# Grouped-query values: each product over 128 keys split into two products over 64 keys, on the upper and lower halves of the array, with the two halves summed after PSUM

## The chip, the cores and the metric

One core of one Trainium2 chip runs the whole program. The metric is device time in microseconds (us) of one execution; lower is better.

## The reference, cut to what matters

The program is a two-layer encoder trunk on 256 tokens of width 1024. Layer 0 uses a dilated attention mixer, layer 1 the windowed grouped-query mixer that the change touches. Each layer runs a SwiGLU block before and after its mixer, and a gated embedding at its end.

```
def reference(x, p, norm_g, ffn_wi, ffn_wo, ple_proj, ple_gate, a_wqkv, a_wo, b_wqkv, b_wo, b_sink, ...):
    for i in range(DEPTH):                      # DEPTH = 2
        h = h + 0.5 * rms_norm(swiglu(rms_norm(h, g[0]), ffn_wi[i, 0], ffn_wo[i, 0]), g[1])
        ...                                     # mixer: dilated (layer 0), window_gqa_mixer (layer 1)
        h = h + 0.5 * rms_norm(swiglu(rms_norm(h, g[4]), ffn_wi[i, 1], ffn_wo[i, 1]), g[5])
        ...                                     # gated embedding

def window_gqa_mixer(h, wqkv, wo, sink, cos, sin):   # 16 heads of 64, 4 key/value heads
    q, k, v = split(h @ wqkv)                        # rope on q and k
    s = q @ k.T / 8, only where |i - j| <= 128
    pr = exp(s - m); den = sum(pr) + exp(sink - m)
    o = (pr @ v) / den                               # the product in question
    return o @ wo
```

## The kernel before

The tokens lie in two tiles of 128 (t = 0, 1). In the grouped-query mixer (`mixer_b`) a unit is one token tile and four heads; there are eight units, (t, pr) with pr = 0 to 3. A unit goes through four steps:

- `scores`: 12 matmuls (L567) of 64 array rows each, alternately on rows 0 to 63 and 64 to 127, into two banks of the pool `psy`. `soft` then adds the mask and takes the row minimum on VectorE (L580), and takes the exponential with its sum on ScalarE (L583).
- `trans`: 16 transposes (`transpose_p`, L340), again 64 rows each and alternating, into two banks of the pool `pst`. ScalarE copies one bank and VectorE the other to `pT` (L343). `pT` has the 128 keys of a key tile on its partitions, and 128 queries in its columns.
- `values`: for each of four heads and each of two key tiles, one fp32 matmul (L602) with `pT` as weights (128 keys x 128 queries) and 64 columns of `V` as the moving side. The trace has two records for each fp32 matmul, so a unit has 16 L602 records; this document calls them the unit's burst. They go to columns 0 to 255 of one bank of the pool `psa`.
- the evacuation: VectorE multiplies by the reciprocal of the denominator (L605), TensorE transposes the result twice (L610) into columns 256 to 511 of the same bank, ScalarE casts it to the output tile `oT` (L73, the high part) and VectorE subtracts (L74, the low part). The bank is free after that subtraction.

The pool `psa` has two banks. A unit takes one of them, so two units alternate. `attend` writes the units down in order, with the scores two units ahead and the transposes one ahead. Output projections (`out_proj`, L205: 48 matmuls of 512 columns for a token tile) are written after unit 4 for t = 0, and at the end for t = 1. A scheduler then sets the order of each engine from that text, with the matmuls of one `scores`, one `transpose_p` kept in their written order. Each engine runs its own list strictly in order. After the mixer the second SwiGLU block of layer 1 follows (L194, L241, L205).

Of the kernel before, what the change touches and what calls it, by code (L numbers as in the profile page):

```python
# [12 lines left out]
ALU = mybir.AluOpType  # L13

P = 128
# [4 lines left out]
DH = 64  # L20
# [17 lines left out]
def trunk_kernel(ctx, tc, x, p, norm_g, ffn_wi, ffn_wo, ple_proj, ple_gate, a_wqkv, a_wo,  # L38
                 b_wqkv, b_wo, b_sink, rope, mask_a, mask_b, out):
    nc = tc.nc  # L40
# [13 lines left out]
    E = mybir.EngineType  # L54
# [7 lines left out]
    def w2_tile(shape, dt=F32):  # L62
        return w2.tile(shape, dt, name="w2t", tag="w2t")

    def m4_tile(shape, dt=F32):
        return m4.tile(shape, dt, name="m4t", tag="m4t")

    def bank(which, shape=(P, 512)):
        pl = {"y": ps_y, "a": ps_a, "t": ps_t}[which]
        return pl.tile(list(shape), F32, name=f"ps{which}", tag=f"ps{which}")  # L70

    def split(dst_hi, dst_lo, src):
        nc.scalar.copy(dst_hi, src)  # L73
        nc.vector.tensor_tensor(dst_lo, src, dst_hi.bitcast(F32), ALU.subtract)  # L74
# [433 lines left out]
    def mixer_b(acts, gb, row):  # L508
# [12 lines left out]
        V = m4_tile([P, 2, 256])  # L521
# [73 lines left out]
        def values(t, pr):  # L595
            a, ih = pr // 2, pr % 2
            pT, rd = pTs.pop((t, pr))
            o_ps = bank("a")
            for n in range(4):
                for kt in range(2):  # L600
                    kv = 2 * a + n % 2
                    nc.tensor.matmul(o_ps[:, n * DH:(n + 1) * DH], pT[:, 2 * n + kt, :],  # L602
                                     V[:, kt, kv * DH:(kv + 1) * DH], start=(kt == 0), stop=(kt == 1))
            o_n = w2_tile([P, 256])
            nc.vector.tensor_tensor(o_n.rearrange("p (n d) -> p n d", d=DH),  # L605
                                    o_ps[:, 0:256].rearrange("p (n d) -> p n d", d=DH),
                                    rd.unsqueeze(2).broadcast_to([P, 4, DH]), ALU.mult)
            pt = o_ps[:, 256:512]
            for i in range(2):
                nc.tensor.transpose(pt[:, i * P:(i + 1) * P], o_n[:, i * P:(i + 1) * P], ident)  # L610
            if ih == 0:
                oT[t, a] = m4_tile([P, 2, 4, P], F32R)
            o = oT[t, a]
            split(o[:, 0, 2 * ih:2 * ih + 2, :].rearrange("p n q -> p (n q)"),
                  o[:, 1, 2 * ih:2 * ih + 2, :].rearrange("p n q -> p (n q)"), pt)
# [22 lines left out]
        def mid():  # L638
            flush()
            score(0)  # L640

        b(1, mid)
        return attend(units, score, trans, values, 1, [lambda k=k: wo_pair(k) for k in range(8)],
                      lambda t: [oT[t, 0], oT[t, 1]], gb, row, flush)

# [82 lines left out]
    start = ExitStack()  # L728
# [83 lines left out]
```

## Time and profile before

| | |
|---|---|
| median of 3 runs | 1082.66 us (1082.51 to 1082.91) |
| the profiled execution | 1083.56 us, of which the span of the trace is 1081.7 us |
| TensorE matmul busy | 1055.7 us, 98% of the span |
| VectorE busy | 692.6 us, 64% |
| ScalarE busy | 565.1 us, 52% |
| mean granted TensorE clock | 0.992 of 2.4 GHz |

The trace's times are microseconds from the start of the span. PE is TensorE's matmul side, PEld its weight loads, DVE is VectorE, ACT is ScalarE. The units' bursts lie between 803.5 and 845 us. Matmuls overlap, so the distance between the starts of two matmuls says more than the duration of one. Nothing below goes by the median alone: a term is found in the profiled execution, and then added to the median.

### The profile page before, as it was taken

How to read it: one execution, taken by the hardware profiler on the slowest of the kernel's cores; microseconds unless marked ns; L12 is line 12 of the kernel's file. 1: busy time of each engine (PE TensorE's matmuls, PEld its weight loads, DVE VectorE, ACT ScalarE, POOL GpSimd, SP SyncE). 2: the span in 40 equal slices, each digit the busy share in tenths (PEclk: the TensorE clock that was granted, in tenths of full speed). 3: DMA queues.
4: the chain of work that ended last, by engine and by line, in shares of the span. 5: the costliest groups of instructions: out<-in, count | busy, mean ns of one | idle time of the engine just before them, and what ended most of it. 6: DMA issues, size and time to landing. Idle time of an engine off the chain costs nothing.

```text
span 1081.7 us, 15005 instructions
## 1 busy us (share of the span) xinstructions
PE 1055.7 (98%) x5254; PEld 862.8 (80%) x5254; DVE 692.6 (64%) x1499; ACT 565.1 (52%) x888; POOL 0.7 (0%) x6
## 2 busy tenths in 40 slices
PE   7999999999999999999999999999999999999996
PEld 5888888778877888888887888888778878888885
DVE  5765554875577856566588654555986866557465
ACT  5654443575576645455456543544674564446343
POOL 0000000000000000000000000000000000000000
PEclk8999999999999999999999999999999999999998
DMA  8965655556550666576444756555651566567501
GB/s 256 298 208 159 212 169 200 175 178 193 175 156 12 202 216 195 160 248 211 160 138 152 232 169 206 180 171 158 179 151 40 168 213 195 168 209 242 200 1 39
DMA packets 130236, 189.05 MB, mean 175 GB/s; under 512 B 9441, under 2 KB 100321, under 8 KB 130161
## 3 DMA queue, kind: packets, MB, share of 16 engines
q1 hardware_dynamic: 130160, 188.10, 54.7%
q8 instruction: 41, 0.67, 0.2%
q14 instruction: 35, 0.28, 0.1%
HBM read 187.02 MB, written 1.05 MB: 174 GB/s over the span
## 4 chain that ended last, share of the span: by engine, by line
PE 92%; DVE 3%; ACT 3%; issue 1%; DMA 1%; SPq 1%; DVEq 0%; ACTq 0%
PE psa L194 55%; PE psy L205 29%; PE pst L241 2%; PE psa L602 1%; PE psa L670 1%; PE pst L147 1%; DMA raw<-in_ffn_wi_dram 1%; PE pst L317 1%; ACT w L88 1%; PE pst L340 1%; ACT w2t L583 1%; PE psa L188 1%; ACT w2t L402 1%; DVE w2t L401 0%; PE psy L326 0%
## 5 line engine op out<-in xcount | busy, mean ns | idle before, releaser
L194 PE MATMUL psa<-w,hgT 128*128 128x512 f32 x2664 | 633.1, 393 | 0.5 <-ACT m4t L380 0.5
L194 PEld LDWEIGHTS psa<-w,hgT 128*128 128x128 f32 x2664 | 494.7, 188 | 103.2 <-ACT m4t L380 0.9
L91 DVE TENSOR_TENSOR w<-raw,w 128x512 fp32r<-128x512 f32 x672 | 435.4, 688 | 168.3 <-ACT w L88 159.6
L88 ACT CAST w<-raw 128x1024 fp32r<-128x1024 f32 (+1 forms) x340 | 352.7, 1042 | 197.0 <-issue 82.8
L205 PE MATMUL psy<-w,w2t 128*128 128x512 f32 x1056 | 260.2, 398 | 2.5 <-ACT w2t L73 2.5
L205 PEld LDWEIGHTS psy<-w,w2t 128*128 128x128 f32 x1056 | 194.4, 188 | 47.4 <-ACT w2t L73 5.4
L232 ACT ACTIVATE w2t<-psa,small 128x256 f32<-128x256 f32 x88 | 41.8, 475 | 155.3 <-PE psa L194 151.0
L233 DVE SCALAR_TENSOR_TENSOR w2t<-psa,small,w2t 128x256 f32<-128x256 f32 x88 | 42.3, 481 | 112.7 <-ACT w2t L232 112.7
L74 DVE TENSOR_TENSOR w2t<-pst,w2t 128x256 fp32r<-128x256 f32 x88 | 36.6, 416 | 9.2 <-ACT w2t L73 9.2
L73 ACT CAST w2t<-pst 128x256 fp32r<-128x256 f32 x88 | 32.2, 366 | 10.1 <-PE pst L241 9.9
L73 ACT CAST hgT<-w2t 128x512 fp32r<-128x512 f32 x32 | 19.5, 620 | 33.7 <-DVE w2t L149 33.5
L205 PE MATMUL psy<-w,m4t 128*128 128x512 f32 x144 | 35.4, 397 | 0.0
L241 PEld LDWEIGHTS pst<-ident,w2t 128*128 128x128 f32 x176 | 24.4, 139 | 13.4 <-issue 1.8
L241 PE MATMUL pst<-ident,w2t 128*128 128x128 f32 x176 | 33.5, 271 | 1.6 <-DVE w2t L233 1.5
L205 PEld LDWEIGHTS psy<-w,m4t 128*128 128x128 f32 x144 | 26.3, 188 | 5.5 <-DVE small L401 0.2
L149 DVE TENSOR_TENSOR w2t<-pst,gcol 128x512 f32<-128x512 f32 x32 | 21.1, 684 | 10.5 <-PE pst L147 10.5
L115 ACT ACTIVATE w2t<-psy 128x512 f32<-128x512 f32 x24 | 14.2, 595 | 18.1 <-DVE w2t L167 18.0
L205 PE MATMUL psy<-w,hgT 128*128 128x512 f32 x96 | 23.4, 392 | 0.0
L172 DVE SCALAR_TENSOR_TENSOR h<-w2t,small,h 128x512 f32<-128x512 f32 x32 | 22.6, 748 | 0.4
L205 PE MATMUL psy<-m4t,hgT 128*128 128x512 f32 x96 | 22.6, 389 | 0.0
L74 DVE TENSOR_TENSOR hgT<-w2t,hgT 128x512 fp32r<-128x512 f32 x32 | 21.4, 687 | 0.9 <-ACT hgT L73 0.4
L167 DVE TENSOR_TENSOR w2t<-psy,gb 128x512 f32<-128x512 f32 x24 | 16.5, 686 | 7.4 <-PE psy L205 7.4
(91 smaller groups left out, 535.0 us busy)
## 6 DMA issues: line engine op xcount, KB each, us to landing
raw<-in_ffn_wi_dram SPq DMA_DIRECT2D x352, 256.0 KB, 4.0
raw<-in_ffn_wo_dram SPq DMA_DIRECT2D x88, 512.0 KB, 4.8
raw<-in_a_wqkv_dram SPq DMA_DIRECT2D x36, 512.0 KB, 4.6
raw<-in_ple_gate_dram SPq DMA_DIRECT2D x16, 512.0 KB, 4.1
raw<-in_b_wqkv_dram SPq DMA_DIRECT2D x12, 512.0 KB, 4.1
gb<-in_norm_g_dram SPq DMA_DIRECT2D x8, 512.0 KB, 4.6
raw<-in_b_wo_dram SPq DMA_DIRECT2D x16, 256.0 KB, 5.8
raw<-in_a_wo_dram SPq DMA_DIRECT2D x4, 512.0 KB, 4.6
```

The costliest lines, as they stand in the source:

```text
L73: nc.scalar.copy(dst_hi, src)
L74: nc.vector.tensor_tensor(dst_lo, src, dst_hi.bitcast(F32), ALU.subtract)
L88: nc.scalar.copy(w[0][:, i:i + step], raw[:, i:i + step])
L91: nc.vector.tensor_tensor(w[1][:, c], raw[:, c], w[0][:, c].bitcast(F32), ALU.subtract)
L149: nc.vector.tensor_tensor(hg, pt.rearrange("p (k q) -> p k q", k=4), gcol[:, 4 * q:4 * q + 4, self.row].unsqueeze(2).broadcast_to([P, 4, P ...
L167: nc.vector.tensor_tensor(g, y[i], gb[:, i * 512:(i + 1) * 512], ALU.mult)
L172: nc.vector.scalar_tensor_tensor(h[t][:, s], yg[i], r, h[t][:, s], ALU.mult, ALU.add)
L194: nc.tensor.matmul(ps, lhs(a, xh, 2 * c + k), ws[c][wh][:, k * 512:(k + 1) * 512], start=(c == 0 and k == 0 and n == 0), stop=(c == 3 and ...
L205: nc.tensor.matmul(y[half], lhsf(k, xh), ws[k][wh][:, half * 512:(half + 1) * 512], start=(first and k == 0 and i == 0), stop=(last and k ...
L232: nc.scalar.activation(su[:, 0, :], ps[:, 0:256], AF.Silu, scale=acts[t].rstd)
L233: nc.vector.scalar_tensor_tensor(su[:, 1, :], ps[:, 256:512], acts[t].rstd, su[:, 0, :], ALU.mult, ALU.mult)
L241: nc.tensor.transpose(pt[:, f * P:(f + 1) * P], su[:, 1, f * P:(f + 1) * P], ident)
```

## The change

```
-            o_ps = bank("a")
-            for n in range(4):
-                for kt in range(2):
-                    kv = 2 * a + n % 2
-                    nc.tensor.matmul(o_ps[:, n * DH:(n + 1) * DH], pT[:, 2 * n + kt, :],
-                                     V[:, kt, kv * DH:(kv + 1) * DH], start=(kt == 0), stop=(kt == 1))
+            o_ps = [bank("a") for _ in range(2)]
+            with tc.manual_schedule(engines={E.PE}):
+                for n in range(4):
+                    for kt in range(2):
+                        for hf in range(2):
+                            kv = 2 * a + n % 2
+                            rows = slice(64 * hf, 64 * hf + 64)
+                            nc.tensor.matmul(o_ps[hf][:, n * DH:(n + 1) * DH], pT[rows, 2 * n + kt, :],
+                                             V[rows, kt, kv * DH:(kv + 1) * DH], start=(kt == 0), stop=(kt == 1))
+            o_h = w2_tile([P, 256])
+            nc.scalar.copy(o_h, o_ps[0][:, 0:256])
             o_n = w2_tile([P, 256])
-            nc.vector.tensor_tensor(o_n.rearrange("p (n d) -> p n d", d=DH),
-                                    o_ps[:, 0:256].rearrange("p (n d) -> p n d", d=DH),
+            nc.vector.tensor_tensor(o_n, o_ps[1][:, 0:256], o_h, ALU.add)
+            nc.vector.tensor_tensor(o_n.rearrange("p (n d) -> p n d", d=DH), o_n.rearrange("p (n d) -> p n d", d=DH),
                                     rd.unsqueeze(2).broadcast_to([P, 4, DH]), ALU.mult)
+            o_ps = o_ps[0]
             pt = o_ps[:, 256:512]
```

Each matmul over 128 keys becomes two over 64 keys, the first on array rows 0 to 63 into one bank, the second on rows 64 to 127 into the other. Both banks of `psa` now belong to one unit. ScalarE copies the first half's sum to SBUF (the copy, L608 of the changed kernel), VectorE adds the second half to it (the add, L610), and multiplies by the reciprocal in SBUF (the multiplication, L611). The transposes of the result (now L616) go to the first bank, as before to the one bank. The matmuls are now L605.

TensorE from unit 1's burst to that of unit 2, before:

```order
L602 MATMUL psa<-m4t,pT 128x64 x8
L340 MATMUL pst<-ident,w2t 128x64 x16
L602 MATMUL psa<-m4t,pT 128x64
L610 MATMUL psa<-ident,w2t 128x128 x2
L602 MATMUL psa<-m4t,pT 128x64 x7
L567 MATMUL psy<-m4t 128x256 x11
```

The same place after the change, on to the burst of unit 2 (the fifteen after the last L567):

```order
L605 MATMUL psa<-m4t,pT 128x64 x15
L340 MATMUL pst<-ident,w2t 128x64 x16
L605 MATMUL psa<-m4t,pT 128x64
L567 MATMUL psy<-m4t 128x256 x6
L616 MATMUL psa<-ident,w2t 128x128 x2
L567 MATMUL psy<-m4t 128x256 x5
L340 MATMUL pst<-ident,w2t 128x64
L567 MATMUL psy<-m4t 128x256
L605 MATMUL psa<-m4t,pT 128x64 x15
```

Before, unit 2's matmuls start right behind the transposes, and unit 1's L610 stands among them. After, only the first matmul of unit 2 stands ahead of unit 1's transposes of the result (it takes the bank that the add frees); the other fifteen stand behind them, since the second one takes the bank that the transposes write.

VectorE around the evacuation of unit 1, after the change (the ISA rows of L580 are the masked minimum and the reading of its result):

```order
L610 TENSOR_TENSOR w2t<-psa,w2t 128x256
L576 COPY w2t<-nsk 128x2
L580 ISA w2t,quad<-psy,msk,nsk 128x256
L580 ISA quad 128x1
L611 TENSOR_TENSOR w2t<-w2t,quad 128x256
L580 ISA w2t,quad<-psy,msk,nsk 128x256
L580 ISA quad 128x1
L576 COPY w2t<-nsk 128x2
L580 ISA w2t,quad<-psy,msk,nsk 128x256
L580 ISA quad 128x1
L74 TENSOR_TENSOR m4t<-psa,m4t 128x256
```

A copy of L576 and one L580 stand between the add and the multiplication, two more L580 between the multiplication and the subtraction that frees the bank. Before, one multiplication from PSUM (L605) stood in place of the add and the multiplication.

TensorE from the transposes of unit 4's result to the end of the first output projection, before:

```order
L602 MATMUL psa<-m4t,pT 128x64 x8
L205 MATMUL psy<-w,m4t 128x512 x7
L610 MATMUL psa<-ident,w2t 128x128 x2
L205 MATMUL psy<-w,m4t 128x512 x39
L567 MATMUL psy<-m4t 128x256 x12
```

The same place after, from the transposes of unit 3's result on:

```order
L605 MATMUL psa<-m4t,pT 128x64
L205 MATMUL psy<-w,m4t 128x512 x3
L616 MATMUL psa<-ident,w2t 128x128 x2
L205 MATMUL psy<-w,m4t 128x512 x5
L605 MATMUL psa<-m4t,pT 128x64 x15
L205 MATMUL psy<-w,m4t 128x512 x6
L616 MATMUL psa<-ident,w2t 128x128 x2
L205 MATMUL psy<-w,m4t 128x512 x32
L567 MATMUL psy<-m4t 128x256 x12
```

Eight of the output projection's matmuls have moved ahead of unit 4's burst (two stand ahead of both pieces in either kernel).

## Rows read from the trace of the kernel before

**Rows 1.** Stages: length, busy PE, PEld, DVE, ACT, POOL (counts), clock, DMA share, GB/s.

```profile
803.50:834.00 30.50, 30.06 (x269) 25.63 (x270) 20.47 (x76) 16.34 (x54) 0.00 (x0) 1.00 0.12 35
834.00:854.00 20.00, 20.00 (x148) 17.25 (x147) 16.86 (x44) 11.88 (x24) 0.00 (x0) 1.00 0.23 67
854.00:1050.00 196.00, 195.62 (x886) 159.53 (x885) 121.57 (x231) 99.21 (x141) 0.00 (x0) 1.00 0.57 185
```

**Rows 2.** Timeline of PE: start, us, line, shapes, count.

```profile
803.52 2.00 PE L602 MATMUL psa<-m4t,pT 128*128 128x64 f32 x16
...
809.37 2.00 PE L602 MATMUL psa<-m4t,pT 128*128 128x64 f32 x16
811.30 0.71 PE L340 MATMUL pst<-ident,w2t 64*128 64x64 f32 x16
811.94 0.43 PE L602 MATMUL psa<-m4t,pT 128*128 128x64 f32 x2
...
816.24 2.00 PE L602 MATMUL psa<-m4t,pT 128*128 128x64 f32 x16
...
820.65 2.00 PE L602 MATMUL psa<-m4t,pT 128*128 128x64 f32 x16
...
824.29 9.13 PE L205 MATMUL psy<-w,m4t 128*128 128x512 f32 x39
```

**Rows 3.** Groups by line and form: busy us, mean ns of one, idle before.

```profile
L602 PEld LDWEIGHTS psa<-m4t,pT 128*128 128x128 f32 x128 | 15.1, 191 | 0.6
...
L340 PEld LDWEIGHTS pst<-ident,w2t 64*128 64x128 f32 x256 | 10.8, 138 | 8.8 <-ACT pT L343 4.6 <-issue 2.9 <-DVE quad L580 0.4
...
L326 PEld LDWEIGHTS psy<-m4t 64*128 64x128 f32 x96 | 7.4, 188 | 1.4 <-issue 1.1
```

**Rows 4.** Timeline of weight loads, bursts of L602 and L340.

```profile
803.52 1.86 PEld L602 LDWEIGHTS psa<-m4t,pT 128*128 128x128 f32 x16
...
808.72 0.58 PEld L340 LDWEIGHTS pst<-ident,w2t 64*128 64x128 f32 x16 [0.58 <-ACT pT L343]
```

**Rows 5.** Timeline of weight loads in layer 0's scores (L326), two short windows.

```profile
295.45 0.30 PEld L326 LDWEIGHTS psy<-m4t 64*128 64x128 f32 x4 [0.35 <-issue]
...
295.99 0.30 PEld L326 LDWEIGHTS psy<-m4t 64*128 64x128 f32 x4
```

**Rows 6.** Timeline of ACT behind unit 0's burst.

```profile
804.75 0.52 ACT L583 ACTIVATE w2t<-w2t,quad 128x257 f32<-128x257 f32 x1
...
806.65 0.19 ACT L583 ACTIVATION_READ_ACCUMULATOR w2t<-w2t,quad 128x1 f32 x1
807.60 0.51 ACT L583 ACTIVATE w2t<-w2t,quad 128x257 f32<-128x257 f32 x1 [0.75 <-DVE quad L580]
```

**Rows 7.** Groups by line and form, 800 to 850 us.

```profile
L580 DVE CUSTOM_DVE_ANT_0 w2t<-psy,msk,nsk 128x256 f32<-128x256 f32 x28 | 12.5, 478 | 0.1
...
L343 DVE COPY pT<-pst 128x512 f32<-128x512 f32 x8 | 5.5, 686 | 0.0
...
L605 DVE TENSOR_TENSOR w2t<-psa,quad 128x256 f32<-128x256 f32 x8 | 3.4, 422 | 1.4 <-PE psa L602 1.1
...
L73 ACT CAST m4t<-psa 128x256 fp32r<-128x256 f32 x8 | 3.0, 372 | 7.7 <-PE psa L610 7.7
```

**Rows 8.** Timeline of all engines behind unit 3's transposes of the result.

```profile
819.76 0.44 PE L610 MATMUL psa<-ident,w2t 128*128 128x128 f32 x2
...
820.24 0.37 ACT L73 CAST m4t<-psa 128x256 fp32r<-128x256 f32 x1 [1.52 <-PE psa L610]
...
820.64 0.42 DVE L74 TENSOR_TENSOR m4t<-psa,m4t 128x256 fp32r<-128x256 f32 x1 [0.86 <-ACT m4t L73]
```

**Rows 9.** Timeline of DVE behind unit 1's burst.

```profile
811.40 0.42 DVE L605 TENSOR_TENSOR w2t<-psa,quad 128x256 f32<-128x256 f32 x1 [0.29 <-PE psa L602]
811.75 0.16 DVE L576 COPY w2t<-nsk 128x2 f32<-128x2 f32 x1
811.81 0.48 DVE L580 CUSTOM_DVE_ANT_0 w2t<-psy,msk,nsk 128x256 f32<-128x256 f32 x1
812.21 0.08 DVE L580 DVE_READ_ACCUMULATOR2_ANT quad<- 128x1 f32 x1
```

## Prediction

> **What bounds the kernel now.** I read the busy time by stage first. From 854 us to near the end PE is busy 195.6 of 196 us at full clock, so whatever the grouped-query stage loses, the rest of the program passes on whole; the stage itself has 0.44 us of idle PE from 803.5 to 834 and none to 854 [rows 1]. PE is the bound, and a change pays only if it shortens PE's list or adds no wait to it.
>
> Second, the timeline of PE. Units' bursts start at 803.52, 809.37, 811.94, 816.24 and 820.65 us [rows 2]: after the first, 2.57, 4.30 and 4.41 us apart, 11.28 us in all. Unit 2's burst starts 2.57 us after unit 1's because the other bank is free; the two-bank pool is what lets PE run on while a result is evacuated.
>
> Third, what sets the pace within a burst. Sixteen weight loads take 1.86 us from the first start to the last end, one lasts 191 ns [rows 3, 4]: (1.86 - 0.191) / 15 = 111 ns from one to the next.
>
> **The change on PE.** 16 records per unit become 32, alternating between two row halves. A non-transposing load of 64 rows lasts 188 ns in layer 0's scores, as good as the 191 ns of 128 rows; a transposing one lasts 138 ns [rows 3]. In those scores, also fp32 in two records and alternating, four loads take 0.30 us: two start together, and the next two (0.30 - 0.188) = 0.11 us later, both early in the burst and later on [rows 5]. So the halves do run side by side, and each half still takes a load every 0.11 us. The lower bound of a pair is that of the transposes: (0.58 - 0.138) / 7 = 63 ns [rows 4]. The upper bound, without any overlap, is 2 x 111 = 222 ns. I take 111 ns, since the load that is to be made has the kind and length of the scores', not that of the transposes. Sixteen pairs at 111 ns are the 1.78 us that sixteen loads of 128 rows take: the split gives PE nothing. It keeps PE in one shape next to L340 and L567 (leaving the burst costs about 0.1 us: 811.30 - 809.37 = 1.93, less 15 x 0.111, leaves 0.26 for the last step and a slow first one [rows 2]), but the bursts near L205 now pay that same price, and where PE waits anyway it saves nothing. I count 0, with -0.6 to +0.4 for the range.
>
> A rule speaks for the change here. The Trainium skill (TensorE: Matmul & The Clock Gate, section "Part 3: Packing small matmuls — row/col tiling") says that a load overlaps a matmul in flight only in another row group. By it the present burst would load and stream in turn, and alternating halves would hide the loads, at about half the price. The trace disagrees: the scores' second loads start 0.11 us after the first on the same rows, while that row group still streams its first product, of 256 keys [rows 5]. By the rule the time would be rival 1's.
>
> **The change in the evacuation.** The multiplication from PSUM (422 ns) becomes a copy on ACT, priced like L73's cast of the same shape (372 ns), an add from PSUM and a multiplication in SBUF (422 ns each, by the same row) [rows 7]. And since a unit holds both banks, the next burst (but for one matmul) stands behind the subtraction that frees the first bank. The chain from burst to burst, with hops of 0.04 us (820.20 to 820.24, 820.61 to 820.64 [rows 8]):
>
> burst 2.00 + hop 0.04 + copy 0.37 + hop 0.04 + add 0.34 (the next DVE instruction starts that much later: 811.40 to 811.75) + L576 0.06 + L580 0.40 [rows 9] + multiplication 0.42 + hop 0.04 + transposes 0.44 + hop 0.04 + cast 0.37 + hop 0.03 + subtraction 0.42 + hop 0.04 [rows 2, 7, 8] = 5.05 us.
>
> Between two bursts PE has, beside the chain's own transposes, only 12 scores (six pairs, 0.67 us by the load pace) and 16 transposes (0.64 us from 811.30 to 811.94 [rows 2]), 1.3 us against the 3.05 us behind the burst. What is queued behind the waiting add on DVE are the minima of the next scores, and behind those ACT's exponentials; PE waits for these last, so they hide in the same gap.
>
> - **Unit 0 to 1.** The copy stands behind four exponentials that end at 806.84 (start 804.75 [rows 6]); ACT idled 0.75 us there, so the copy itself is free. Copy to about 807.0, add to 807.45; then L576, one L580 and the copy of `pT` (0.60 to the next start, of 0.69 [rows 7]) stand ahead of the multiplication: 807.06 + 0.34 + 0.06 + 0.40 + 0.60 = 808.46, end 808.9. Transposes, cast and subtraction with their hops: 808.9 + 1.4 = 810.3, against a burst at 809.37 [rows 2]: **+0.95**.
> - **Units 1 to 4.** Three periods of 5.05, with 0.1 us more in two of them where PE changes shape on the chain: 15.35 against 11.28 [rows 2]: **+4.1**.
> - **Given back.** Eight of the output projection's matmuls now run in those gaps instead of after unit 4, at (9.13 - 0.4) / 38 = 0.23 us each [rows 2]: **-1.8**.
> - **Units 5 to 7.** The second `pT` bank of the next unit is freed by an ACT copy that now stands behind the new copy, and so behind unit 5's burst: about 0.8 us of waiting, by estimate 2.0 + 0.4 + 0.6 us of burst and copies less the 2 us of transposes and matmuls that PE has. The last units run among L205: their gaps are filled, but each is entered and left twice (one matmul, then fifteen), two shape changes more than before and four restarts, some 0.9 us. After the last burst 3.05 us of chain face nine L205 (2.1 us) and five L194 before the rest can run, and ACT has 1 us weight casts in its list: 0.5 us. Together **+2.2** (1 to 3.5).
>
> Sum: 0.95 + 4.1 - 1.8 + 2.2 = **+5.45 us**. On the profiled execution that is 1083.56 + 5.45 = 1089.0 us (span 1087.1). That execution lies 0.9 us above the median of the runs; on the median the same sum gives **1088.1 us**.
>
> **The rivals.**
> 1. *The row halves load at the transposes' price.* A burst falls by 16 x (111 - 63) = 0.77 us. Unit 0 to 1 stays +0.95 (ACT sets it); three periods give 15.35 - 2.3 = 13.0, +1.8; units 4 to 7 save 0.77 each, 3.1; with -1.8 and +2.2 the sum is about 0: 1082.7, and 1085 if DVE's minima and weight halves, which then stand ahead of the add, eat the shorter burst. This is the case that ends "not slower"; it decides for that from a pair below about 80 ns, where 3.3 of the 5.45 us are gone. For it: 64 x 128 transposes with 64 columns at 63 ns [rows 4]. Against: 188 and not 138 ns per load [rows 3].
> 2. *No overlap at all.* 1.78 us more for each of eight bursts, 14.2 us, less some waits: about 1101. Against it stand paired loads in both windows [rows 5].
> 3. *The chain is longer than I count*: semaphore hops with two waits, an L91 weight half (0.69 us) ahead of an add, or a lower clock in the gaps. At 0.4 us more in eight units: 1091.3. The clock stays 1.00 in all these stages [rows 1], so I give the clock little.
>
> **How the numbers follow.** Forecast case 0.66 (1086 to 1090.5), rival 1 0.15, rival 2 0.04, rival 3 0.11, a gain from something not listed 0.04. A measurement here tells 0.2% (2.2 us) from no change. Rival 1 puts about 0.11 within that and 0.02 on either side; so faster 0.06, the same 0.11, slower 0.83. The range from 1084.0 to 1091.8 leaves out half of rival 1, rival 2, the gain and the ends of rival 3.
>
> **What the profile would show.** Right: 256 records of L605, paired, 16 pairs in about 2 us; starts of units 2, 3 and 4 some 5 us apart; PE idle from 803.5 to 834 grown from 0.4 to some 4 us, its releasers DVE's subtraction and multiplication (L74, L611); L73 behind L616 on ACT; the same clock; stages after the mixer shifted, not changed. Wrong: bursts near 1 us (rival 1) or near 3.6 us (rival 2), or periods near 4.3 us, which would mean that I mistook what the second bank waits for.

## The result

The changed kernel takes 1096.45 us (median of 4 runs, 1094.62 to 1098.46), the kernel before 1082.59 us on the same chip (4 runs, 1082.34 to 1082.91): ratio 1.0124, 95% interval 1.0111 to 1.0138, so 13.9 us slower. Forecast were 1088.1 us and a range to 1091.8 us: the sign was right, the time lies outside. The mean granted clock of the four runs is 0.980 to 0.991. The profiled execution is one of them: 1098.46 us, span 1096.7 us, 15.0 us above the span before.

The stages of the changed kernel, with the columns of [rows 1] (the last column but two is the granted clock):

```profile
803.50:834.00 30.50, 29.32 (x271) 25.32 (x270) 19.25 (x75) 16.32 (x53) 0.00 (x0) 0.61 0.13 35
834.00:854.00 20.00, 19.33 (x170) 15.93 (x168) 10.00 (x34) 7.29 (x24) 0.00 (x0) 0.99 0.01 2
854.00:1050.00 196.00, 195.94 (x924) 159.44 (x923) 123.30 (x229) 98.84 (x140) 0.00 (x0) 1.00 0.60 192
...
803.50:810.48 6.98, 5.89 (x90) 4.85 (x88) 6.80 (x28) 5.67 (x18) 0.00 (x0) 1.00 0.21 50
810.49:834.38 23.89, 23.81 (x184) 20.75 (x183) 12.82 (x49) 11.01 (x37) 0.00 (x0) 0.50 0.10 30
```

Where [rows 1] show a clock of 1.00, the first stage has 0.61: for 23.89 us, from 810.49 to 834.38, TensorE ran at 1.2 instead of 2.4 GHz. Its busy time in that stretch is 23.81 us. PE barely idles there; it is slow. The idle time that I had forecast, some 4 us in the first stage, comes to 1.18 us, and 1.09 us of it lie ahead of that stretch, from 803.50 to 810.48. Behind it the clock is back, and from 854 us on PE is as busy as before.

This trace has one more fall of the clock, in layer 0, whose code the change does not touch. The first row is of the changed kernel, the second of the same place in the kernel before:

```profile
318.94:322.35 3.41, 3.41 (x40) 2.85 (x39) 2.06 (x7) 1.52 (x4) 0.00 (x0) 0.50 0.74 289
...
316.00:325.00 9.00, 7.23 (x126) 6.26 (x122) 5.74 (x15) 6.68 (x14) 0.00 (x0) 1.00 0.68 218
```

Ahead of it PE had waited 1.56 us and had then run transposes (L340) and scores (L326) of 64 rows. Such a short fall, then, is not peculiar to the change; the long one is what the time has to be explained by.

The timeline of PE, with the bursts of the units (compare [rows 2]):

```profile
803.80 2.02 PE L605 MATMUL psa<-m4t,pT 64*128 64x64 f32 x32
...
809.13 0.40 PE L340 MATMUL pst<-ident,w2t 64*128 64x64 f32 x6 [0.78 <-DVE pT L343]
809.46 0.44 PE L616 MATMUL psa<-ident,w2t 128*128 128x128 f32 x2
...
810.81 3.46 PE L605 MATMUL psa<-m4t,pT 64*128 64x64 f32 x29
...
818.04 3.46 PE L605 MATMUL psa<-m4t,pT 64*128 64x64 f32 x29
...
826.27 3.46 PE L605 MATMUL psa<-m4t,pT 64*128 64x64 f32 x29
...
834.90 2.00 PE L605 MATMUL psa<-m4t,pT 64*128 64x64 f32 x30
...
847.23 1.95 PE L605 MATMUL psa<-m4t,pT 64*128 64x64 f32 x32
...
866.24 1.69 PE L194 MATMUL psa<-w,hgT 128*128 128x512 f32 x5
867.77 2.89 PE L205 MATMUL psy<-w,m4t 128*128 128x512 f32 x12
870.50 1.75 PE L194 MATMUL psa<-w,hgT 128*128 128x512 f32 x7
```

A burst of 32 records takes 2.02 us at full clock, as 16 did before, and 29 of them take 3.46 us at half clock. The starts of units 1, 2, 3 and 4 are 7.23, 8.23 and 8.63 us apart, 24.09 in all.

The chain behind unit 0's burst, on ACT and DVE (against [rows 6] and [rows 8]):

```profile
807.18 0.36 ACT L608 COPY w2t<-psa 128x256 f32<-128x256 f32 x1
807.58 0.42 DVE L610 TENSOR_TENSOR w2t<-psa,w2t 128x256 f32<-128x256 f32 x1
808.99 0.41 DVE L611 TENSOR_TENSOR w2t<-w2t,quad 128x256 f32<-128x256 f32 x1
...
810.34 0.42 DVE L74 TENSOR_TENSOR m4t<-psa,m4t 128x256 fp32r<-128x256 f32 x1
```

The copy, add and multiplication have the forecast durations. The subtraction ends at 810.76, and at 810.81 the burst of unit 1 goes on, now at half clock.

Two rows of the timeline of PE before are wanted below, unit 5's burst and the first L194 behind the mixer:

```profile
834.76 2.00 PE L602 MATMUL psa<-m4t,pT 128*128 128x64 f32 x16
...
854.07 8.32 PE L194 MATMUL psa<-w,hgT 128*128 128x512 f32 x36
```

### The profile page after: what moved, and what is told of

The parts are those of the page before. It is cut to its first block, busy times and chain, and to the rows that moved or that the text cites. A ratio compares the mean times of both kernels' runs of the same rounds, so it can differ in the third digit from the quotient of the medians.

```text
span 1096.7 us, 15277 instructions
## 1 busy us (share of the span) xinstructions
PE 1069.6 (98%) x5382; PEld 873.4 (80%) x5382; DVE 696.1 (63%) x1507; ACT 568.3 (52%) x896; POOL 0.7 (0%) x6
## 4 chain that ended last, share of the span: by engine, by line
PE 91%; DVE 3%; ACT 3%; issue 1%; DMA 1%; SPq 1%; DVEq 0%; ACTq 0%
PE psa L194 54%; PE psy L205 29%; PE pst L241 2%; PE psa L605 2%; PE psa L676 1%; PE pst L147 1%; DMA raw<-in_ffn_wi_dram 1%; ACT w L88 1%; PE pst L340 1%; PE pst L317 1%; PE psa L188 1%; ACT w2t L583 1%; ACT w2t L402 1%; DVE w2t L401 0%; PE psy L326 0%
## 5 line engine op out<-in xcount | busy, mean ns | idle before, releaser
L194 PE MATMUL psa<-w,hgT 128*128 128x512 f32 x2664 | 633.7, 393 | 0.6 <-ACT m4t L380 0.5
L194 PEld LDWEIGHTS psa<-w,hgT 128*128 128x128 f32 x2664 | 494.5, 188 | 103.8 <-DVE hgT L74 1.0
L205 PE MATMUL psy<-w,w2t 128*128 128x512 f32 x1056 | 260.1, 398 | 2.5 <-ACT w2t L73 2.5
L205 PEld LDWEIGHTS psy<-w,w2t 128*128 128x128 f32 x1056 | 194.3, 188 | 47.3 <-ACT w2t L73 5.4
L205 PE MATMUL psy<-w,m4t 128*128 128x512 f32 x144 | 39.2, 417 | 0.0
L205 PEld LDWEIGHTS psy<-w,m4t 128*128 128x128 f32 x144 | 26.9, 197 | 6.0 <-ACT m4t L73 0.2
L605 PEld LDWEIGHTS psa<-m4t,pT 64*128 64x128 f32 x256 | 22.2, 240 | 2.9 <-DVE m4t L74 1.1
L605 PE MATMUL psa<-m4t,pT 64*128 64x64 f32 x256 | 24.3, 330 | 0.1
L205 PE MATMUL psy<-w,hgT 128*128 128x512 f32 x96 | 23.4, 393 | 0.0
L205 PE MATMUL psy<-m4t,hgT 128*128 128x512 f32 x96 | 22.6, 389 | 0.0
```

What stands on the lines that cost most here:

```text
L194: nc.tensor.matmul(ps, lhs(a, xh, 2 * c + k), ws[c][wh][:, k * 512:(k + 1) * 512], start=(c == 0 and k == 0 and n == 0), stop=(c == 3 and ...
L205: nc.tensor.matmul(y[half], lhsf(k, xh), ws[k][wh][:, half * 512:(half + 1) * 512], start=(first and k == 0 and i == 0), stop=(last and k ...
L605: nc.tensor.matmul(o_ps[hf][:, n * DH:(n + 1) * DH], pT[rows, 2 * n + kt, :], V[rows, kt, kv * DH:(kv + 1) * DH], start=(kt == 0), stop=(k ...
```

## Experiments

Two theories first. A: the waits did it (two banks held, a longer chain), the split is neutral, and idle PE let the clock fall. B: the products on 64 rows did it. The second group adds C: it takes both, 64-row products and the waits of the copy and the add. Kernels of one group ran on one chip, each group on another. Before's runs there: 1081.17 to 1084.30 us (15 runs, median 1082.69) in the first group, 1081.46 to 1085.04 (27, 1082.75) in the second, 1081.11 to 1083.47 (15, 1082.17) in the third. Some kernels have two kinds of runs, told apart by their times and mean clocks, so both stand beside the medians. Only one run of each kernel has a trace, and the mean clock takes in the start and the end of the program too, where the clock is low as well (0.50 from 10 to 15 us in the trace of before); a fall as short as 3.4 us can't be read from it.

### First group: waits or rows

**e1_keytiles** keeps the whole chain of the change (two banks, copy, add, multiplication), but with products of 128 rows (against the change):

```
-                        for hf in range(2): ... o_ps[hf] <- pT[rows, ...], V[rows, ...], start=(kt == 0), stop=(kt == 1)
+                        o_ps[kt] <- pT[:, ...], V[:, ...], start=True, stop=True
```

> Full 128-row products as before, but the two key tiles go to two banks, with the copy, the add and the multiplication of the change: same banks, same evacuation, no row split. Theory A (the waits from the held banks and the longer evacuation let the TensorE clock fall, the row split is neutral): half clock again for 10 to 25 us behind unit 1's burst, 1091 to 1098 us, starts of units 2 to 4 over 6 us apart. Theory B (the 64-row products are what lets the clock fall): clock 1.00 throughout the mixer, periods near 5 us, 1087 to 1089 us.

Measured: 1086.49 us (5 runs, 1085.76 to 1086.95), ratio 1.0032 (1.0020 to 1.0045), clock 0.991 to 0.997. Its stage and its timeline of PE:

```profile
803.50:834.00 30.50, 29.04 (x255) 24.30 (x252) 21.63 (x82) 18.09 (x59) 0.00 (x0) 1.00 0.12 35
```

```profile
803.88 2.00 PE L603 MATMUL psa<-m4t,pT 128*128 128x64 f32 x16
...
809.04 0.40 PE L340 MATMUL pst<-ident,w2t 64*128 64x64 f32 x6 [0.78 <-DVE pT L343]
809.37 0.44 PE L614 MATMUL psa<-ident,w2t 128*128 128x128 f32 x2
...
810.87 1.77 PE L603 MATMUL psa<-m4t,pT 128*128 128x64 f32 x14
...
815.82 1.77 PE L603 MATMUL psa<-m4t,pT 128*128 128x64 f32 x14 [0.38 <-DVE m4t L74]
...
821.08 1.67 PE L603 MATMUL psa<-m4t,pT 128*128 128x64 f32 x14
...
825.77 1.71 PE L603 MATMUL psa<-m4t,pT 128*128 128x64 f32 x14
```

Up to 810.87 this timeline is that of the changed kernel within 0.1 us, waits included, and PE is idle for longer in the stage (1.46 us); yet the clock stays at 1.00, and none of the five runs has a low mean clock. Theory A falls: the waits alone do not lower it. The time is slightly below theory B's range. The periods, 4.95, 5.26 and 4.69 us, are the chain that I had worked out.

**e2_twobanks** holds both banks too, with 128-row products and no sum: heads of even number to one bank, of odd number to the other, two multiplications (the products' line):

```
+                        o_ps[n % 2] <- pT[:, 2 * n + kt, :], V[:, kt, ...], start=(kt == 0), stop=(kt == 1)
```

> Full 128-row products; the heads of a unit are divided between two banks, so a unit holds both banks of the pool but nothing is copied or added: two multiplications of 128 columns in place of one of 256. Theories A and B alike expect a shorter chain (no copy, no add: about 0.8 us less) and so 1083 to 1086 us at full clock. If holding both banks were enough for the clock to fall, over 1090 us.

Measured: 1083.01 us (11 runs, 1081.99 to 1083.99), ratio 1.0004 (0.9995 to 1.0013). The two banks cost nothing that this can tell by themselves; the longer chain through them does (e1_keytiles, +3.5 us).

**e4y_bank_y** is the change, with the second half's bank from the scores' pool.

```
-            o_ps = [bank("a") for _ in range(2)]
+            o_ps = [bank("a"), bank("y")]
```

> The change, but the second half's bank comes from the pool of the scores (four banks), so that two units alternate in the pool psa as before: row split, copy, add and multiplication stay, the wait for the bank goes. Theory A: full clock and 1083 to 1087 us, with some waits of scores for their banks. Theory B: the clock falls all the same, over 1090 us.

Measured: 1098.36 us (4 runs, 1096.53 to 1098.90), ratio 1.0140 (1.0126 to 1.0154), clock 0.976 to 0.980. The clock falls sooner, 1.75 us after the first product of unit 0 (804.68), and stays low for longer, so the wait for the second bank is not what lowers it:

```profile
806.43:837.15 30.72, 30.16 (x274) 27.17 (x272) 19.58 (x72) 15.36 (x54) 0.00 (x0) 0.50 0.12 35
```

**e3_fill** is the change with the first score pass issued four times, 12 more 64-row products a unit.

```
-                    for n, (x, y) in enumerate(PASSES):
+                    for n, (x, y) in [(-1, PASSES[0])] * 3 + list(enumerate(PASSES)):
...
-                                             kT[y][rows, a, :], start=(n == 0), stop=(n == 2))
+                                             kT[y][rows, a, :], start=(n <= 0), stop=(n < 0 or n == 2))
```

> The change, with the first pass of each score product issued four times instead of once (12 more 64-row matmuls of 256 columns a unit, the result unchanged): work of 0.7 us a unit on PE, most of it in the gaps. Theory A: the clock holds at 1.00 and the time falls below that of the change although work is added, 1087 to 1092 us. Theory B (64-row products let the clock fall): no better than the change, 1096 us or more.

Measured: 1096.86 us (4 runs, 1094.70 to 1097.51), ratio 1.0126 (1.0110 to 1.0141). Its stretches at half clock are down to two of 3.4 us:

```profile
803.50:834.00 30.50, 25.32 (x357) 22.73 (x356) 20.32 (x76) 16.16 (x55) 0.00 (x0) 0.94 0.12 36
814.11:817.52 3.41, 3.41 (x44) 3.41 (x42) 2.54 (x10) 1.84 (x8) 0.00 (x0) 0.50 0.02 5
848.24:851.66 3.42, 3.42 (x24) 2.44 (x23) 1.81 (x5) 1.53 (x5) 0.00 (x0) 0.50 0.02 5
```

PE idles 5.18 us in the first of these rows, so the fill does not cover the waits but adds to them. The time is the one that theory B gave, but not for its reason: 6.83 us at half clock cost at most 3.4 us, by estimate, of the 13.6 us that this kernel is slower than the one before (0.0126 x 1082.7). With the work and the waits both changed, it says little on the theories.

### Second group: the rows by themselves

**e8_lowrows** is the kernel before with one edit, which leaves half of the keys out of the sum. Every engine keeps its list, instruction for instruction.

```
-                    ... pT[:, 2 * n + kt, :], V[:, kt, kv * DH:(kv + 1) * DH], ...
+                    ... pT[0:64, 2 * n + kt, :], V[0:64, kt, kv * DH:(kv + 1) * DH], ...
```

> The kernel before, with one edit: its 16 products of a unit use only the lower 64 keys of each key tile (rows 0 to 63 of the array); the upper 64 keys are left out of the sum. Every engine keeps its list of instructions word for word, one bank a unit and one evacuation. If a load of 64 rows takes the pace of one of 128 (0.11 us), as the split bursts showed, the pace is that of before. Theory B: clock falls somewhere in the mixer, 1085 to 1094 us. Theory C: full clock, 1082.3 to 1083.3 us. A gain over 0.5 us would show that 64-row products alone are cheaper than I read.

Measured: 12 runs, 1081.39 to 1093.95 us, median 1083.37. Seven lie at 1081.39 to 1084.21 us with a mean clock of 0.989 to 0.996, five at 1091.41 to 1093.95 us with 0.979 to 0.987. None of the 57 runs of before passed 1085.04 us. The profiled execution is one of the seven, and even it has a short fall, right behind unit 0's burst (which starts at 801.77):

```profile
800.00:804.03 4.03, 3.79 (x36) 3.15 (x35) 4.03 (x21) 4.03 (x14) 0.00 (x0) 1.00 0.01 3
804.04:807.45 3.41, 3.41 (x36) 2.97 (x36) 3.09 (x13) 2.66 (x11) 0.00 (x0) 0.50 0.02 5
807.46:834.00 26.54, 26.54 (x248) 23.10 (x245) 16.95 (x65) 13.30 (x46) 0.00 (x0) 1.00 0.13 40
```

PE is busy for 3.79 of the 4.03 us ahead of the fall and never idles from 804.04 on. Half the rows in the values' products alone, with no wait added, are enough for some runs to be slow at a low mean clock, which none of before's 27 on this chip is. A gain of 64-row products as such is not to be seen: the fastest runs lie at the fastest of before.

**e7_split_nosum** has the split products and both banks, but no copy and no add (two multiplications as in e2_twobanks). Against e2_twobanks:

```
-                        o_ps[n % 2] <- pT[:, 2 * n + kt, :], V[:, kt, ...]
+                        for hf in range(2): o_ps[hf] <- pT[rows, 2 * n + kt, :], V[rows, kt, ...]
```

> The change's products as they are (32 of 64 rows per unit, both banks taken), but without copy and add: the multiplication reads the heads of even number from the first bank and those of odd number from the second, in two instructions of 128 columns as in e2_twobanks. This leaves the other 64 keys of each key tile out of each head's sum. Against e2_twobanks, which ran at full clock in 1083.0 us, only the split of the products is new. Theory B (the 64-row products let the granted clock fall, with or without the longer evacuation): a stretch at half clock in the mixer and 1086 to 1095 us. Theory C (it takes both, 64-row products and the waits of the copy and the add): clock full and 1082.5 to 1084.5 us.

Measured: 12 runs, median 1087.26 us: ten at 1084.79 to 1088.37 us (clock 0.990 to 0.997) and two at 1095.41 and 1097.85 us (0.984 and 0.980). The profiled execution is the slowest of the ten, 1088.37 us, and it has a short fall too, behind unit 5's burst, with the first stage at 1.00:

```profile
803.50:834.00 30.50, 29.61 (x341) 25.04 (x338) 19.78 (x83) 16.20 (x54) 0.00 (x0) 1.00 0.12 36
840.47:843.88 3.41, 3.41 (x16) 2.46 (x13) 1.70 (x4) 0.74 (x2) 0.00 (x0) 0.50 0.03 7
```

Theory C falls: it does not take the chain for the clock to fall. But only 2 runs of 12 show a loss like the change's. Where the profiled run has its full clock, from unit 0's burst (803.84) to unit 5's (836.47), the split costs 32.63 against 31.24 us in the kernel before, 1.4 us, and the two banks of e2_twobanks 0.4 (803.47 to 835.07).

**e9_fullfill** is the change, with six products of 128 rows for nothing ahead of each unit's scores.

```
                 for i in range(2):
+                    for _ in range(3):
+                        nc.tensor.matmul(s[i][:, 0:256], qT[a][0][:, 2 * ih + i, t * P:(t + 1) * P],
+                                         kT[0][:, a, :], start=True, stop=True)
+                for i in range(2):
...
```

> The change, with six further products of all 128 rows (256 columns, the scores' shape) ahead of each unit's scores, written into the scores' banks and overwritten by them: work for nothing that fills PE's waits with full rows, some 0.7 us a unit. In e3_fill the same time of 64-row work shortened the half clock to two stretches of 3.4 us, and cost what it saved. Theory B or C (what counts is how much of the array works): no half clock in the mixer or one stretch at most, and the time falls to 1087 to 1092 us, the price of the chain plus up to 4 us of fill in the units where PE does not wait. If the clock still falls for over 10 us, the fill's rows do not matter and 1095 to 1099 us is to be seen.

Measured: 1092.59 us (4 runs, 1092.23 to 1093.08), ratio 1.0090 (1.0077 to 1.0103), clock 0.993 to 0.998. The stage at full clock, though PE idles 2.1 us in it:

```profile
803.50:834.00 30.50, 28.41 (x348) 24.52 (x348) 20.60 (x77) 16.60 (x57) 0.00 (x0) 1.00 0.11 36
```

More work made the kernel faster than the change without it, by 3.7 us (ratio 1.0090 against 1.0124, each to the kernel before beside it). The idle time stayed, the traced run has its full clock, and none of the four has a low mean clock; the time lies a little above the forecast 1092. That it is the rows of the fill, and not the added work as such, is not quite separated: the 64-row fill of e3_fill had cut the half clock too, from 23.89 to 6.83 us, though it added idle time.

**e6_t0only** has the change only in the four units of token tile 0.

> The change for the four units of token tile 0 alone; those of tile 1 keep the 128-row products, one bank and one multiplication. The half clock of the changed kernel lies from 810.5 to 834.4 us, over the units of tile 0 and the first of tile 1. Theory B or C (the loss comes where split products and their waits stand among other 64-row work): half clock stays, and 1091 to 1097 us. If it is the eight units together that count, the clock falls for a shorter time or not at all: 1085 to 1088 us, the price of the chain in three periods less what the output projection gives back.

Measured: 10 runs in two kinds: five at 1084.70 to 1087.68 us (clock 0.989 to 0.998), five at 1094.40 to 1095.65 us (0.980 to 0.985). The profile is of the first kind, and shows the chain of split products at full clock:

```profile
808.55 1.89 PE L606 MATMUL psa<-m4t,pT 64*128 64x64 f32 x29
...
813.49 1.88 PE L606 MATMUL psa<-m4t,pT 64*128 64x64 f32 x29 [0.25 <-DVE m4t L74]
...
818.69 1.88 PE L606 MATMUL psa<-m4t,pT 64*128 64x64 f32 x29
```

4.94 and 5.20 us apart: this is the term as I had priced it (5.05, and 5.15 with a change of shape). The low runs have no trace.

### Third group: rows or data, and what is left at full clock

**e12_zerokeys** sums the same keys as e8_lowrows, but with all 128 rows in use (against the kernel before):

```
                 nc.scalar.activation(V[:, t, :], ps[:, 256:512], AF.Copy, scale=acts[t].rstd)
+                nc.gpsimd.memset(V[64:128, t, :], 0.0)
```

> The kernel before with one edit: the upper 64 keys of V's tiles are set to zero on GpSimd, which is otherwise idle, so the products sum the same keys as in e8_lowrows, but with 128 rows of weights and 128 rows of moving data. Again the upper 64 keys are left out of the sum, and TensorE's list is that of before. In e8_lowrows 5 of 12 runs took 1091.4 to 1094.0 us at a mean clock of 0.979 to 0.987. Theory D (what counts is how many rows of the array an instruction uses): all runs at 1081.4 to 1085 us, as before. Theory E (what counts is how much of the data is at work, as a draw of current would have it): some runs at 1090 to 1094 us and a clock below 0.988.

Measured: 1082.74 us (11 runs, 1081.99 to 1083.40), ratio 1.0005 (0.9996 to 1.0014), clock 0.992 to 0.998 in every run. None of 11 is low, where e8_lowrows had 5 of 12. This speaks for theory D: the rows that the instruction uses count, not whether the moving data in them are zero (the weights were not). One rival is left: e8_lowrows ran on another chip, and on this chip no kernel had low runs, so it is not shown that this chip would have let the clock fall.

**e11_keyfill** is e1_keytiles with the fill of e9_fullfill.

> e1_keytiles (products of 128 rows, one key tile to a bank, with copy, add and multiplication; 1086.5 us) with the six further products of 128 rows ahead of each unit's scores as in e9_fullfill (1092.6 us, no half clock). Against e9_fullfill only the split into 64 rows is missing. If the split costs nothing but the clock: 1091.5 to 1093.5 us, the same as e9_fullfill, and the fill's own price is some 6 us. If the 64-row products cost time at full clock as well: 1087 to 1090 us.

Measured: 1088.57 us (5 runs, 1088.14 to 1090.10), ratio 1.0065 (1.0051 to 1.0079), clock 0.992 to 0.998. So the split costs time at full clock as well, 2.7 us by the ratios (1.0090 - 1.0065), and the fill costs about 3.5 us and not 6 (ratio 1.0065 against 1.0032 of e1_keytiles); both figures are uncertain by some 2 us, by the intervals. In the traces 2.0 us of it lie between unit 0's burst and unit 5's, where both kernels run the same 48 L205: 803.29 to 838.60 us here, 35.31, and 803.79 to 841.07 in e9_fullfill, 37.28. Part of that is order: here seven L205 stand ahead of unit 4's burst, there none.

**e6_t1only** has the change only in the four units of token tile 1.

> The change for the four units of token tile 1 alone, three of which stand among the output projection's products of 128 rows; those of tile 0 keep the 128-row products. e6_t0only had two kinds of runs, 1084.7 to 1087.7 us and 1094.4 to 1095.7 us. If the clock falls where little else than 64-row work runs: no run at half clock for long, and 1083 to 1086 us (my +2.2 us for units 5 to 7 and no periods of 5 us). If any split product does it: runs at 1090 us or more here too.

Measured: 1085.29 us (5 runs, 1085.21 to 1087.17), ratio 1.0033 (1.0021 to 1.0046), clock 0.992 to 0.993. No run at a low clock: among the 128-row products of the output projection the split products cost 3.1 us. That too was measured on the chip on which no kernel had low runs.

The runs in one table; "low" are runs above 1090 us with a mean clock under 0.988, and rows are those of the values' products.

| kernel | rows | chain of the sum | low runs |
|---|---|---|---|
| before | 128 | no | 0 of 57 |
| e2_twobanks, e12_zerokeys | 128 | no | 0 of 22 |
| e1_keytiles, e11_keyfill | 128 | yes | 0 of 10 |
| e8_lowrows | 64, low half only | no | 5 of 12 |
| e7_split_nosum | 64 | no | 2 of 12 |
| e6_t0only | 64 in units 0 to 3 | yes, there | 5 of 10 |
| e6_t1only | 64 in units 4 to 7 | yes, there | 0 of 5 |
| e4y_bank_y | 64 | yes | 4 of 4 |
| e9_fullfill | 64, with 128-row fill | yes | 0 of 4 |

The changed kernel's four runs have 0.980, 0.981, 0.988 and 0.991 at 1098.46, 1098.17, 1094.62 and 1094.72 us: all far from the 1089 us that the next section estimates for full clock, but by mean clock not all low. The four of e3_fill, 0.987 to 0.993 at 1094.70 to 1097.51 us, lose more to added work and waits than to the clock, as far as the traced one tells.

## Why the prediction was wrong

- **The change on PE: right for the burst.** 16 pairs take what 16 loads took (2.02 against 2.00 us with the last one's drain), so the split gives PE nothing. Rival 1, a burst at half the price, was seen in no run. The bursts of 3.46 us look like rival 2's 3.6, but they stand at half clock; those of units 0, 4 and 5 take 2.02, 2.00 and 1.95 us. Beyond the burst the split does cost something, where I had put 0 (-0.6 to +0.4): 1.4 us over five units in e7_split_nosum, 2.7 us in all between the two fill kernels.
- **Unit 0 to 1: right.** 810.81 - 803.80 = 7.01 against 5.85 [rows 2], +1.16 where I had +0.95.
- **Units 1 to 4: the step that failed.** "Three periods of 5.05 ... 15.35 against 11.28: +4.1" was measured at 834.90 - 810.81 = 24.09, which is +12.8. The chain was right (4.94 and 5.20 in e6_t0only, 4.95, 5.26 and 4.69 with full rows in e1_keytiles), but I priced it at the clock of the kernel before. All three periods ran at 1.2 GHz, where PE is busy almost throughout (23.81 of 23.89 us): its own list, slowed by the clock, sets the pace in place of the chain, and the eight L205 that were to fill waits take their time as well.
- **Given back: right.** Unit 4 to 5 takes 847.23 - 834.90 = 12.33 against 834.76 - 820.65 = 14.11: -1.78, forecast -1.8.
- **Units 5 to 7: right within its bounds.** The mixer's matmuls end at 870.50 less the five L194 that went ahead (5 x 0.23), 869.35, so 22.1 us after unit 5's burst, before 854.07 - 834.76 = 19.3: +2.8, forecast +2.2 (1 to 3.5).

The four terms are 1.16 + 12.81 - 1.78 + 2.8 = 15.0 us, the difference of the two spans. With 4.1 in the place of 12.8 the sum is 6.3 us. The runs agree by two other ways, both estimates. e9_fullfill less the fill's own price is 1.0090 - (1.0065 - 1.0032) = 1.0057, or 6.2 us over before at full clock, uncertain by some 2.5 us. And the two halves of the change alone cost 3.1 us (e6_t1only) and 3.3 us (the five faster runs of e6_t0only, median 1086.00 against 1082.75), 6.4 together. So of 13.9 us some 6 are what I had summed up as 5.45, and some 8 are the clock's; in the profiled run it is 8.7 of 15.0, and in the two runs at 1094.6 to 1094.7 us nearer to 6.

The sentence behind the failed step is in rival 3: "The clock stays 1.00 in all these stages, so I give the clock little". [rows 1] show that clock for the kernel before, where the scores and the transposes of the same stage already use 64 rows; the bursts, with 128, made up most of the rest up to 824 us, where the L205 begin in number. I took a clock at its full level for a margin. I also would have looked for the cause in the idle time ("a lower clock in the gaps"), and e1_keytiles shows that idle time alone does not lower it, while e8_lowrows shows the clock falling with no wait added.

What is shown: without full rows in the bursts the clock can fall, and on the chips of the first two groups none of the runs with them was low, whatever the waits; the five such kernels with a trace have 1.00 throughout the mixer (89 runs in all, with those of the third group). What stays open is whether zeros in the data matter, on a chip that is known to fall, and why a given run of e7_split_nosum, e8_lowrows or e6_t0only falls and the next one doesn't, and how much the chain adds to the risk: with 64 rows in all units, 7 of 24 runs were low without it, and every run of e4y_bank_y with it. The low runs of e8_lowrows, e7_split_nosum and e6_t0only are known by times and mean clocks only, since the profiled runs were not among them. No version beat the kernel before, since the split has nothing to give on PE.

## What to carry over

Where small matmuls use half of the array's rows, a busy share near 100% at full clock does not say how far the clock is from falling; before you halve the rows of the last full-row products among them, price the stage at half clock too. A split of a full 128-row contraction into two row halves gives no PE time here, and its sum needs a copy, an add and a second bank, which turns a pool of two banks into a chain from one unit to the next. Test a suspected clock by what the array does, and not only by what it waits for: full rows for nothing made the changed kernel faster, and of two kernels with the same waits the one with half rows was slow.

## What the runs showed of the hardware

- The granted clock stayed at 0.50 while PE was busy for 23.81 of 23.89 us (the change), and it fell behind 4.03 us of which PE was busy for 3.79 (e8_lowrows). Busy time was no guard against it.
- The same list of TensorE's instructions, with 64 instead of 128 rows in 128 of its records, had 5 low runs of 12; with 128 rows and half of the moving data zeros, none of 11, on another chip.
- The length of the fall differs: 3.41 us (e8_lowrows, e7_split_nosum, and layer 0 in the changed kernel's trace), 23.89 us (the change), 30.72 us (e4y_bank_y).
- Pairs of 64-row fp32 products on the two row halves follow each other every 0.11 us (16 pairs in 2.02 us), as single products of 128 rows do (16 in 2.00 us).
